# Hybrid encoder trunk on one core: the attention's first tiles on the memory of the decays and shifts, stores of the rotated queries on other queues, the S5 parameters in two parts

## The chip, the cores and the metric

One core of a Trainium2 chip runs the whole layer as one program. The metric is the device time of one execution in microseconds (us). The engines are TensorE (PE, with its weight loads PEld), VectorE (DVE), ScalarE (ACT), GpSimd (POOL) and SyncE (SP, which here only issues DMAs). ACT and POOL can issue DMAs too; each engine's DMAs go out in the order of its own instructions.

## The reference, cut to what matters

One post-norm layer for two groups of tokens that share the weights: 1024 prompt frames and 32 new frames of a running stream (T = 1056 columns).

```python
proj = x @ w_in                       # q_lat 256 | kv_lat 128 | k_rope 32 | u 256 | rwkv 1280
q = rms_norm(q_lat) @ w_qb            # 6 heads x (64 nope + 32 rope), rope columns rotated
ckv = rms_norm(kv_lat); krope = rope(k_rope)
kv = concat(ckv_past, ckv) @ w_kvb    # k_nope and v; past: 512 frames
mla = softmax((q_nope k_nope + q_rope k_rope) * scale) v        # chunk-causal
s5  = glu(S5 recurrence of u)         # parameters: powers of exp(lam * dt), B, C
rwkv = RWKV-7 recurrence of mixes ps = p + (prev - p) * mu      # r, k, v, decay, a, gate
x = layer_norm(alpha * x + concat(mla, s5, rwkv) @ w_out)
x = layer_norm(alpha * x + square(relu(x @ w_up)) @ w_down)
```

All matrix products keep fp32 accuracy: an operand is split into a high and a low part, and three matmuls (high x high, low x high, high x low) take the place of one.

## The kernel before, in words

The program has three stretches. **The input phase** (0 to some 307 us) projects x by column blocks. `in_proj` is 72 matmuls: 8 contraction tiles, three pieces of columns (384, 384 and 288), three matmuls each (lines 63, 65 and 67). `tile_trunk` runs in turn: the input and its split; the S5 parameters (`stage_s5_params`: products `tb` on POOL at line 530, their sum `bl` on VectorE at line 531, four groups of transposes of `bl` on TensorE at line 537, then tables of powers on VectorE, lines 577 to 596); the mix for the low-rank gates and the three k streams; `stage_lora` (line 277); `front_k` for the three pairs of heads (scans of the log decays at line 374 with the mask `m65`, normalisation, the pair products on TensorE at line 725 with their transposes at line 731); the value and receptance streams (`stage_mixed` with q = 2 and 0); the kv latent, the rope key, the q latent and its normalisation; `stage_q`, six products `scq` of q with evictions on ACT (line 1158) and the rotation on POOL (lines 1179 to 1188), stored to the scratch `q_d`; and `stage_u`, two in-projections.

A stream is one `in_proj`, its eviction to `raw` on ACT (lines 225 to 228), a difference on POOL (line 238) and `mix` on VectorE (line 239).

**The middle** (to some 800 us) is the attention beside the two recurrences. `rwkv_inv` is a generator: a substitution of 31 steps on VectorE (lines 759 and 760) up to its yield, then a copy `zt` on ACT, stores to scratch and loads back, and products on TensorE between the attention's (line 786). `side_by_side` alternates steps of the attention (a) and of the streams (b): LEAD steps of a, one of b, then RATIO of a for each of b. The attention starts with `attn_past` (past latents `ct` and past rope keys `kt` are loaded and transposed, lines 1076 and 1082) and `attn_setup` (the keys' rope rows `kr`, the key products `sck` at line 1117, all split into `kh` on ACT and `kl` on VectorE). Rows 96 to 127 of the keys hold a zero block with a row of -1 in it. A `q` of a head is loaded from `q_d` and split into `qh` and `ql`; then scores `sc` come.

**The MLP** is the rest.

A list scheduler sets the order on each engine from the dependencies, with priorities (`high_priority`) and with `issue_after`, which holds a step behind a named instruction. Tiles come from pools, which lie on one another as on a stack. In pools with `reuse_waits="tile"` a new tile waits for the last users of the tiles whose memory it takes; in the others it waits for the pool below.

Of the kernel before, what the change touches and what calls it, by code (L numbers as in the profile page):

```python
# [17 lines left out]
P = 128  # L18
# [392 lines left out]
def stage_s5_params(g, sp):  # L411
# [120 lines left out]
    V.tensor_copy(out=blv[:, :, 7], in_=bbv[0])  # L532
    em = big("em")[:, :2048].rearrange("p (g x) -> p g x", x=P)
# [208 lines left out]
def rwkv_inv(g):  # L742
# [319 lines left out]
RATIO, LEAD, PRIO = 2.5, 24, 120  # L1062
# [3 lines left out]
def attn_past(g):  # L1066

    nc = g.nc
    g.wkv = g.ap0.tile([P, 2, 384], F32, tag="wkv", name="wkv")
    nc.sync.dma_start(out=g.wkv, in_=g.a["w_kvb"])  # L1070
    g.cpast = g.ap0.tile([P, 512], F32, tag="cpast", name="cpast")
    ct = g.ap.tile([P, 4, P], F32, tag="rec", name="ct", bufs=1)
    nc.sync.dma_start(out=ct, in_=g.a["ckv0"].rearrange("(t p) c -> p t c", p=P))
    ps = g.pst.tile([P, 4, P], F32, tag="st", name="sct")
    for t in range(4):
        nc.tensor.transpose(out=ps[:, t], in_=ct[:, t], identity=g.ident)
    nc.scalar.activation(out=g.cpast, in_=ps.rearrange("p t x -> p (t x)"), func=AF.Copy)
    kt = g.ap.tile([P, 4, 32], F32, tag="rt", name="kt", bufs=1)
    nc.sync.dma_start(out=kt, in_=g.a["kr0"].rearrange("(t p) c -> p t c", p=P))
    ps = g.pst.tile([P, 4, P], F32, tag="st", name="sct")  # L1080
    for t in range(4):
        nc.tensor.transpose(out=ps[:32, t], in_=kt[:, t], identity=g.ident)
    g.kpast = g.ap0.tile([P, 512], F32, tag="kpast", name="kpast")[64:96]
    nc.scalar.activation(out=g.kpast, in_=ps[:32].rearrange("p t x -> p (t x)"), func=AF.Copy)


def attn_setup(g):

    nc = g.nc
# [12 lines left out]
    nc.gpsimd.memset(kr[96:97], -1.0)
    split3(g, kr[64:128], g.kh[0][64:128], g.kl[0][64:128])
# [37 lines left out]
def stage_q(g):  # L1141
# [33 lines left out]
    qa = f("qrope")  # L1175
    qs = g.p1.tile([P, 1152], F32, tag="kk", name="qturn", bufs=3)[:, :T]
# [7 lines left out]
    qb, qt = (g.p1.tile([P, 1152], F32, tag="kk", name=x, bufs=3)[:, :T] for x in ("qropeb", "qturnb"))  # L1184
# [110 lines left out]
def side_by_side(g, a, b):  # L1295
# [3 lines left out]
    n, done = LEAD, [False, False]  # L1299
# [335 lines left out]
def tile_trunk(ctx, tc, a, o):  # L1635
# [29 lines left out]
    with ExitStack() as s1:  # L1665
        g.pacc = s1.enter_context(tc.tile_pool(name="pacc", bufs=3, space=PSUM))
        g.pt = s1.enter_context(tc.tile_pool(name="pt", bufs=2, space=PSUM))
        g.wpool = s1.enter_context(tc.tile_pool(name="wpool", bufs=2))
        xp = s1.enter_context(tc.tile_pool(name="xp", bufs=1))
# [5 lines left out]
        g.rawp = s2.enter_context(tc.tile_pool(name="rawp", bufs=1, reuse_waits="tile"))  # L1675
# [4 lines left out]
        lp = s2.enter_context(tc.tile_pool(name="lp", bufs=1, reuse_waits="tile"))  # L1680
        g.at = lp.tile([P, 3, WSH], F32, tag="at", name="at")
        g.cs65 = lp.tile([P, 3, 1073], F32, tag="cs65", name="cs65")
        with tc.tile_pool(name="lq", bufs=1, side="right", reuse_waits="tile") as g.lq:
            with tc.tile_pool(name="s5p", bufs=1, side="right", reuse_waits="tile") as sp:
                stage_s5_params(g, sp)
# [4 lines left out]
            g.lmix = mixed(g, raw_in(g, 3, 9, w=w0), 9)  # L1690
            for p in PAIRS:
                stage_mixed(g, p, 1, w=w1 if p == PAIRS[0] else None)
            stage_lora(g)
# [24 lines left out]
    inv = rwkv_inv(g)  # L1718
    next(inv)
# [143 lines left out]
```

## Time and profile before

| | |
|---|---|
| median of 3 runs | 1632.05 us (1631.82 to 1632.66) |
| the profiled execution | 1634.02 us, span 1632.2 us, 1.8 us around it |
| mean granted TensorE clock | 0.954 |
| busy: PE, DVE, ACT, POOL | 1501.1, 916.5, 512.4, 413.4 us |
| PE's waits of one kind over 7 us in all | `sck` on VectorE 14.9, `pra` on ACT 12.1, `sct` on a DMA 8.4, `av` on POOL 8.3, `acc` on ACT 7.6, `acc` on VectorE 7.2 |

The busy times overlap between engines. A row of a timeline gives the start, the duration, the engine and the line, what is written and read, and in brackets how long the engine stood idle before and what released it. The durations of neighbouring matmuls overlap; their pace is the distance of the starts. SPq and ACTq are the DMA issues of these engines. Clock 1.00 is the full TensorE clock.

### The profile page before, as it was taken

To read this page: it belongs to the slowest core of one execution; us is meant where nothing else is said; L and a number is where in the kernel's file an instruction comes from. 1 tells how busy PE (TensorE), PEld (TensorE's weight loads), DVE (VectorE), ACT (ScalarE), POOL (GpSimd) and SP (SyncE) were. 2 spreads that over 40 slices of the span, in tenths; PEclk is the share of its full clock that TensorE was granted. 3 is DMA by queue.
4 is the path that set the end of the run, shared out by engine and by line. 5 is a ranking of instruction groups with operands and counts; after the bars stand their busy time and mean duration, and the time that the engine had idled before them with its cause. 6 is when DMAs were issued, how large, how long until landed. Compare 5 with 4: busy or idle time off the path is not lost. (4 is left out here: it accounts for less than half of the span.)

```text
span 1632.2 us, 26334 instructions
## 1 busy us (share of the span) xinstructions
PE 1501.1 (92%) x10855; PEld 1348.1 (83%) x10855; DVE 916.5 (56%) x1674; ACT 512.4 (31%) x990; POOL 413.4 (25%) x386
## 2 busy tenths in 40 slices
PE   7899889688899868989799999999999999999995
PEld 6789778466667556657678999999999999999995
DVE  8467958163566534454766755544554545445457
ACT  5434434313554534443223122221111122221122
POOL 3614551622111011121412112221211122212123
PEclk9979999868999989989999999999999999999998
DMA  5314452707233231122612111111111111111012
GB/s 181 124 64 172 139 140 68 186 15 117 61 92 93 58 82 42 60 77 79 204 53 91 39 40 52 52 39 52 40 52 39 39 52 53 51 41 52 14 39 82
DMA packets 112669, 123.50 MB, mean 76 GB/s; under 512 B 51328, under 2 KB 87860, under 8 KB 112168
## 3 DMA queue, kind: packets, MB, share of 16 engines
q1 hardware_dynamic: 93092, 103.64, 21.8%
q10 hardware_dynamic: 19392, 17.97, 3.5%
q8 instruction: 85, 1.39, 0.3%
q14 instruction: 36, 0.29, 0.1%
q0 software_dynamic: 64, 0.20, 0.0%
HBM read 89.05 MB, written 32.68 MB: 75 GB/s over the span
## 5 line engine op out<-in xcount | busy, mean ns | idle before, releaser
L63 PE MATMUL acc<-xh,uphi 128*128 128x384 f32 (+1 forms) x768 | 248.9, 324 | 0.0
L65 PE MATMUL acc<-xl,uphi 128*128 128x384 f32 (+1 forms) x768 | 247.9, 323 | 0.0
L67 PE MATMUL acc<-xh,uplo 128*128 128x384 f32 (+1 forms) x768 | 247.6, 322 | 0.0
L1533 DVE TENSOR_TENSOR rl<-rl 128x384 f32<-128x384 f32 (+1 forms) x96 | 142.1, 1481 | 176.5 <-ACT rl L1532 175.1
L1561 DVE TENSOR_TENSOR yacc<-yacc,acc 128x384 f32<-128x384 f32 (+2 forms) x344 | 158.7, 507 | 111.6 <-PE acc L67 111.6
L63 PE MATMUL acc<-hh,dnhi 128*128 128x384 f32 (+2 forms) x736 | 209.3, 320 | 0.0
L65 PE MATMUL acc<-hl,dnhi 128*128 128x384 f32 (+2 forms) x736 | 207.1, 319 | 0.0
L67 PE MATMUL acc<-hh,dnlo 128*128 128x384 f32 (+2 forms) x736 | 197.4, 319 | 0.0
L50 POOL TENSOR_TENSOR dnlo<-dnraw,dnhi 128x1024 fp32r<-128x1024 f32 x30 | 72.6, 2421 | 337.3 <-ACT dnhi L49 322.1
L63 PEld LDWEIGHTS acc<-xh,uphi 128*128 128x128 f32 x768 | 144.1, 188 | 0.3 <-ACT xh L49 0.3
L67 PEld LDWEIGHTS acc<-xh,uplo 128*128 128x128 f32 x768 | 144.3, 188 | 0.0
L65 PEld LDWEIGHTS acc<-xl,uphi 128*128 128x128 f32 x768 | 144.2, 188 | 0.0
L50 POOL TENSOR_TENSOR uplo<-upraw,uphi 128x1024 fp32r<-128x1024 f32 x34 | 82.3, 2421 | 237.9 <-ACT uphi L49 237.7
L63 PE MATMUL acc<-xh,wmhi 128*128 128x384 f32 (+3 forms) x384 | 134.3, 350 | 8.5 <-ACT xh L49 7.6
L65 PE MATMUL acc<-xl,wmhi 128*128 128x384 f32 (+3 forms) x384 | 134.3, 350 | 2.6 <-DVE xl L50 2.5
L67 PE MATMUL acc<-xh,wmlo 128*128 128x384 f32 (+3 forms) x384 | 133.2, 347 | 0.0
L65 PEld LDWEIGHTS acc<-hl,dnhi 128*128 128x128 f32 x736 | 131.5, 188 | 0.0
L63 PEld LDWEIGHTS acc<-hh,dnhi 128*128 128x128 f32 x736 | 131.4, 188 | 0.0
L67 PEld LDWEIGHTS acc<-hh,dnlo 128*128 128x128 f32 x736 | 128.9, 188 | 0.0
L49 ACT ACTIVATE dnhi<-dnraw 128x1024 fp32r<-128x1024 f32 x30 | 31.8, 1060 | 299.4 <-PE acc L65 249.2
L49 ACT ACTIVATE hh<-rl 128x384 fp32r<-128x384 f32 (+1 forms) x96 | 47.9, 499 | 148.7 <-DVE rl L1533 148.7
L63 PEld LDWEIGHTS acc<-xh,wmhi 128*128 128x128 f32 (+1 forms) x384 | 75.8, 197 | 14.1 <-ACT xh L49 7.9
(484 smaller groups left out, 2897.1 us busy)
## 6 DMA issues: line engine op xcount, KB each, us to landing
upraw<-in_w_up SPq DMA_DIRECT2D x32, 512.0 KB
dnraw<-in_w_dn SPq DMA_DIRECT2D x30, 512.0 KB, 3.6
ld<-rw SPq DMA_DIRECT2D x24, 320.0 KB, 5.8
wmraw<-in_w_m SPq DMA_DIRECT2D x12, 512.0 KB, 4.9
wo<-in_w_out SPq DMA_DIRECT2D x8, 512.0 KB, 4.0
z<-in_xa SPq DMA_DIRECT2D x8, 512.0 KB
out_y<-o SPq DMA_DIRECT2D x8, 512.0 KB, 2.6
xr<-in_xt SPq DMA_DIRECT2D x8, 384.0 KB, 6.5
```

The lines of the kernel that those rows point to most:

```text
L49: nc.scalar.activation(out=hi, in_=ps, func=AF.Copy)
L50: (lo_eng or nc.vector).tensor_tensor(out=lo, in0=ps, in1=hi.bitcast(F32), op=ALU.subtract)
L63: nc.tensor.matmul(out=outs[i], lhsT=lh, rhs=rhs[i][0], start=start, stop=False)
L65: nc.tensor.matmul(out=outs[i], lhsT=lh, rhs=rhs[i][1], start=False, stop=False)
L67: nc.tensor.matmul(out=outs[i], lhsT=ll, rhs=rhs[i][0], start=False, stop=stop)
L1533: nc.vector.tensor_tensor(out=r[:, :n], in0=r[:, :n], in1=r[:, :n], op=ALU.mult)
L1561: nc.vector.tensor_tensor(out=y, in0=y, in1=ps[i][:, :n], op=ALU.add)
```

## The change

Five things change.

1. Pools. `pt` comes below `pacc`; all pools of the phase get `reuse_waits="tile"`. The decays `cs65` and shifts `at`, and then `raw` and `mix`, move to the bottom of the stack, where the attention's first tiles will lie. `ut` leaves `raw`'s pool for `p1`. `p1` (tiles of the k pairs, the mask `m65`) opens when both the S5 and the lora pools have closed.
2. `stage_s5_params` yields ahead of the transposes of `bl`; the rest is issued behind the last matmul of the lora mix and the three k streams.
3. `rwkv_inv` gets a second yield behind the substitution, whose text now stands right behind `front_k`. `zt` and its stores come in the first step of b; the stores go to SP's queue, behind the last SP instruction. LEAD becomes 10, then 14.
4. `attn_past` takes its PSUM from `psc`. `kr` is one tile of 1056 columns with one load, and the keys' rope rows are split from three pieces (past 512, prompt 1024, new 32), with no copy of the past ones into `kr`.
5. `stage_q`: both products of heads 0 to 3's rope columns first, then the first nope product, the rope product of heads 4 and 5, and the other nope products. The nope stores go to ACT's queue, the rope stores to POOL's.

```diff
-        ut = g.rawp.tile([P, L5, NC5], F32, tag="mix", name="ut", bufs=2)
+        ut = g.p1.tile([P, L5, NC5], F32, tag="f", name="ut", bufs=5)
...
     V.tensor_copy(out=blv[:, :, 7], in_=bbv[0])
+    yield
     em = big("em")[:, :2048].rearrange("p (g x) -> p g x", x=P)
...
+    yield
     zt = g.ip.tile([H, 32, 32], F32, tag="nn", name="zt", bufs=1)
     nc.scalar.activation(out=zt, in_=y[:, 0].rearrange("u i a -> u a i"), func=AF.Copy)
-    nc.scalar.dma_start(out=g.zt_d, in_=zt)
-    nc.scalar.dma_start(out=g.xt_d[:, 0:2], in_=y)
+    nc.sync.dma_start(out=g.zt_d, in_=zt)
+    nc.sync.dma_start(out=g.xt_d[:, 0:2], in_=y)
...
-RATIO, LEAD, PRIO = 2.5, 24, 120
+RATIO, LEAD, PRIO = 2.5, (10, 14), 120
...
-    ps = g.pst.tile([P, 4, P], F32, tag="st", name="sct")
+    ps = g.psc.tile([P, 4, P], F32, tag="sc", name="sct")
...
-    kr = g.ap.tile([P, 1568], F32, tag="vo", name="kr", bufs=1)
-    nc.sync.dma_start(out=kr[64:96, 0:TP], in_=g.kr_d[:, 0:TP])
-    nc.sync.dma_start(out=kr[64:96, 1536:1568], in_=g.kr_d[:, TP:T])
-    nc.scalar.activation(out=kr[64:96, 1024:1536], in_=g.kpast, func=AF.Copy)
-    nc.gpsimd.memset(kr[96:128], 0.0)
-    nc.gpsimd.memset(kr[96:97], -1.0)
-    split3(g, kr[64:128], g.kh[0][64:128], g.kl[0][64:128])
+    nc.sync.dma_start(out=kr[64:96], in_=g.kr_d)
+    for x in (kr, g.kpast):
+        nc.gpsimd.memset(x[96:128], 0.0)
+        nc.gpsimd.memset(x[96:97], -1.0)
+    for x, o, c, n in ((g.kpast, TP, 0, 512), (kr, 0, 0, TP), (kr, 1536, TP, TS)):
+        split3(g, x[64:128, c:c + n], g.kh[0][64:128, o:o + n], g.kl[0][64:128, o:o + n])
...
-            nc.sync.dma_start(out=g.q_d[2 * p + h, 0:64], in_=q[hsl(h)])
+            nc.scalar.dma_start(out=g.q_d[2 * p + h, 0:64], in_=q[hsl(h)])
...
+    nope(0)
     for h in range(4):
-        nc.sync.dma_start(out=g.q_d[h, 64:96], in_=qa[32 * h:32 * h + 32])
+        nc.gpsimd.dma_start(out=g.q_d[h, 64:96], in_=qa[32 * h:32 * h + 32])
     product(qb, wr[:, :, 2])
...
+    nope(1)
+    nope(2)
     for h in range(2):
-        nc.sync.dma_start(out=g.q_d[4 + h, 64:96], in_=qb[32 * h:32 * h + 32])
+        nc.gpsimd.dma_start(out=g.q_d[4 + h, 64:96], in_=qb[32 * h:32 * h + 32])
...
+                params = stage_s5_params(g, sp)
+                next(params)
+                g.lmix = mixed(g, raw_in(g, 3, 9, w=w0), 9)
+                for p in PAIRS:
+                    stage_mixed(g, p, 1, w=w1 if p == PAIRS[0] else None)
+                with tc.issue_after(last_traced(g, mybir.EngineType.PE)):
+                    next(params, None)
+                stage_lora(g)
             g.p1 = s2.enter_context(tc.tile_pool(name="p1", bufs=1, reuse_waits="tile"))
...
         for p in PAIRS:
             front_k(g, p)
+        inv = rwkv_inv(g)
+        next(inv)
```

The scheduler's order moves at three places. On TensorE, around the transposes of `bl` (names without `bl` are in-projection matmuls, `fs` is the lora). Before:

```order
L63 MATMUL acc<-xh,wmhi 128x384
L65 MATMUL acc<-xl,wmhi 128x384
L67 MATMUL acc<-xh,wmlo 128x384
L537 MATMUL pt<-ident,bl 128x128 x8
L63 MATMUL acc<-xh,wmhi 128x384
L65 MATMUL acc<-xl,wmhi 128x384
```

Now:

```order
L63 MATMUL acc<-xh,wmhi 128x288
L65 MATMUL acc<-xl,wmhi 128x288
L67 MATMUL acc<-xh,wmlo 128x288
L538 MATMUL pt<-ident,bl 128x128 x8
L277 MATMUL fs<-lah,wh 128x384
L277 MATMUL fs<-lal,wh 128x384
```

252 in-projection matmuls stood ahead of the transposes before; now all 288 of the first four streams do. Two streams later the same order has one more thing: VectorE's scans (line 374) stood behind the mix of the second value stream and now stand behind the third's, and the first product that reads them (line 316) has 612 in-projection matmuls ahead of it instead of 555.

On SP's queue, where the attention's first loads stand. Before:

```order
L1070 DMA wkv<-in_w_kvb 128x768
L1183 DMA q_d<-qrope 32x1056 x4
L1073 DMA ct<-in_ckv 128x4x128
L1079 DMA kt<-in_kr 128x4x32
L1098 DMA kr<-kr_d 32x1024
L1099 DMA kr<-kr_d 32x32
L1198 DMA q<-q_d 96x1056
```

Now (`in_w_u` are weights of the last in-projections; `wkv` stands four rows higher):

```order
L55 DMA wmraw<-in_w_u 128x1024
L1075 DMA ct<-in_ckv 128x4x128
L1081 DMA kt<-in_kr 128x4x32
L1100 DMA kr<-kr_d 32x1056
L936 DMA st<-in_s 128x3x64
L628 DMA ces<-tab_d 128x2x536
L983 DMA gate<-rw_61 128x32
L983 DMA gate<-rw_62 128x32
L983 DMA gate<-rw_63 128x32
L1202 DMA q<-q_d 96x1056
L765 DMA zt_d<-zt 108x1024
```

No store of q stands on this queue any more, and the stores of the inverse stand behind the first load of a `q`.

On POOL, from the rotation of q to the attention's clearings. Before:

```order
L1181 TENSOR_TENSOR qrope<-qrope,qturn 128x1056
L1186 TENSOR_TENSOR qturnb<-qropeb,ropes 64x1056
L1187 TENSOR_TENSOR qropeb<-qropeb,ropec 64x1056
L1101 MEMSET kr 32x1568
L1213 MEMSET mx 128x18 x2
L637 MEMSET ces 128x8
L1188 TENSOR_TENSOR qropeb<-qropeb,qturnb 64x1056
L1102 MEMSET kr 1x1568
L1109 TENSOR_TENSOR qh<-kr 32x1056
```

Now:

```order
L1183 TENSOR_TENSOR qrope<-qrope,qturn 128x1056
L1189 TENSOR_TENSOR qropeb<-qropeb,ropec 64x1056
L1186 DMA q_d<-qrope 32x1056 x4
L1188 TENSOR_TENSOR qturnb<-qropeb,ropes 64x1056
L1190 TENSOR_TENSOR qropeb<-qropeb,qturnb 64x1056
L1194 DMA q_d<-qropeb 32x1056 x2
L1102 MEMSET kr 32x1056
L1217 MEMSET mx 128x18 x2
L1130 MEMSET vo 128x13x64
L638 MEMSET ces 128x8
L1103 MEMSET kr 1x1056
L1111 TENSOR_TENSOR qh<-kr 32x1056
```

The clearing of `kr` now stands behind six DMA issues. On TensorE the products of q stood among the 72 matmuls of the last `u`; now all of them stand ahead of these.

## Rows read from the trace of the kernel before

**Rows 1.** Windows of the span: busy us of each engine, PE clock, DMA share, GB/s.
```profile
63.30:68.00 4.70, 4.70 (x20) 4.70 (x21) 0.28 (x1) 1.19 (x2) 4.38 (x4) 0.60 0.28 92
...
246.00:307.10 61.10, 60.99 (x312) 51.12 (x310) 34.08 (x58) 23.11 (x49) 12.72 (x5) 1.00 0.40 108
307.10:333.50 26.40, 7.46 (x17) 3.52 (x16) 13.92 (x13) 9.94 (x18) 25.95 (x17) 0.61 0.53 157
...
800.00:1600.00 800.00, 798.50 (x4954) 781.96 (x4953) 435.52 (x698) 176.14 (x326) 171.77 (x83) 1.00 0.16 49
```

**Rows 2.** Waits of TensorE over the whole span: us in total, times, longest us.
```profile
PE sck L1117 <- DVE kl L50: 14.9, 5, 7.4
...
PE sct L1076 <- DMA ct<-in_ckv: 8.4, 1, 8.4
```

**Rows 3.** Timeline of TensorE around the transposes of `bl`.
```profile
53.71 0.34 PE L67 MATMUL acc<-xh,wmlo 128*128 128x384 f32 x1
53.89 0.34 PE L63 MATMUL acc<-xh,wmhi 128*128 128x384 f32 x1
...
63.23 1.97 PE L537 MATMUL pt<-ident,bl 128*128 128x128 f32 x8 [6.02 <-DVE bl L531]
```

**Rows 4.** Timeline of VectorE, the sum `bl`.
```profile
57.63 5.55 DVE L531 TENSOR_TENSOR bl<-bl,tb 128x1792 f32<-128x1792 f32 x1 [3.56 <-POOL tb L530]
```

**Rows 5.** Timeline of VectorE, the scans and the mix ahead.
```profile
137.54 1.31 DVE L239 SCALAR_TENSOR_TENSOR mix<-mix,vec,raw 128x1058 f32<-128x1058 f32 x1
139.62 11.36 DVE L374 TENSOR_TENSOR_SCAN cs<-m,cs 128x260 f32<-128x260 bf16 x14 [0.77 <-POOL m L1689]
```

**Rows 6.** Timeline of ACT, last evictions of the second and third value streams.
```profile
130.44 0.19 ACT L228 ACTIVATE raw<-acc 128x32 f32<-128x32 f32 x1
...
144.46 0.19 ACT L228 ACTIVATE raw<-acc 128x32 f32<-128x32 f32 x1
```

**Rows 7.** Timeline of TensorE, the first pair products.
```profile
178.64 1.16 PE L725 MATMUL fs<-fc,fq 64*64 64x64 f32 x64 [1.66 <-DVE fq L344]
```

**Rows 8.** Timeline of SP, its DMA issues after the input phase.
```profile
307.65 3.55 SPq L1183 DMA_DIRECT2D q_d<-qrope  x4
311.25 0.51 SPq L1073 DMA_DIRECT2D ct<-in_ckv  x1
```

**Rows 9.** Timeline of TensorE, start of the attention.
```profile
315.56 1.09 PE L1076 MATMUL sct<-ident,ct 128*128 128x128 f32 x4 [8.44 <-DMA ct<-in_ckv]
...
333.55 0.44 PE L63 MATMUL sc<-kh,qh 128*128 128x128 f32 x1 [1.72 <-DVE kl L50]
```

**Rows 10.** Window of the q products alone (PE, PEld, ACT; clock, DMA share, GB/s).
```profile
269.94:307.10 37.16, 23.62 (x72) 12.93 (x72) 7.91 (x18) 1.00 0.54 145
```

**Rows 11.** Timeline of POOL, rotation of q, clearing of `kr`, rows of `qh`.
```profile
299.88 2.44 POOL L1179 TENSOR_TENSOR qrope<-qrope,ropec 128x1056 f32<-128x1056 f32 x1 [37.28 <-ACT qturn L1158]
...
312.31 1.40 POOL L1101 MEMSET kr<- 32x1568 f32 x1
...
317.86 1.94 POOL L1109 TENSOR_TENSOR qh<-kr 32x1056 fp32r<-32x1056 f32 x1
```

**Rows 12.** Groups of POOL: busy us, mean ns, idle before, releaser.
```profile
L1733 POOL DMA_DIRECT2D mg_d<-yc x1 | 0.9, 942 | 0.3 <-POOL yc L992 0.3
```

**Rows 13.** Timeline of ACT, the split of `kr`.
```profile
321.14 1.51 ACT L49 ACTIVATE kh<-kr 64x1568 fp32r<-64x1568 f32 x1
```

**Rows 14.** Timeline of VectorE, residuals of q and of the keys.
```profile
318.72 4.01 DVE L50 TENSOR_TENSOR ql<-q,qh 96x512 fp32r<-96x512 f32 x2 [37.54 <-ACT qh L49]
322.66 0.67 DVE L50 TENSOR_TENSOR kl<-sck,kh 64x512 fp32r<-64x512 f32 x1
323.36 2.83 DVE L50 TENSOR_TENSOR kl<-kr,kh 64x1568 fp32r<-64x1568 f32 x1
```

**Rows 15.** Instructions on the mixes: durations ns, first and last start us.
```profile
L344 POOL TENSOR_TENSOR mix<-mix,cs x6: 240/1784/3149, 201.3 to 218.3; 128x1024 f32<-128x1024 f32 x3, 128x32 f32<-128x32 f32 x3
...
L337 ACTq DMA_DIRECT2D rw<-mix x3: 397/397/443, 206.6 to 221.3; - x3
```

More of the change, by code (lines that the diff above doesn't have):

```diff
@@ L1079, in attn_past @@
     nc.sync.dma_start(out=kt, in_=g.a["kr0"].rearrange("(t p) c -> p t c", p=P))
-    ps = g.pst.tile([P, 4, P], F32, tag="st", name="sct")
+    ps = g.psc.tile([P, 4, P], F32, tag="sc", name="sct")
     for t in range(4):
         nc.tensor.transpose(out=ps[:32, t], in_=kt[:, t], identity=g.ident)
-    g.kpast = g.ap0.tile([P, 512], F32, tag="kpast", name="kpast")[64:96]
-    nc.scalar.activation(out=g.kpast, in_=ps[:32].rearrange("p t x -> p (t x)"), func=AF.Copy)
+    g.kpast = g.ap0.tile([P, 512], F32, tag="kpast", name="kpast")
+    nc.scalar.activation(out=g.kpast[64:96], in_=ps[:32].rearrange("p t x -> p (t x)"), func=AF.Copy)
 def attn_setup(g):
@@ L1090, in attn_setup @@
     g.kh, g.kl, g.q2 = [], [], []
+    kr = g.ap.tile([P, T], F32, tag="q", name="kr", bufs=1)
     for i in range(NKT):
@@ L1165, in stage_q, with nope @@
             nc.scalar.dma_start(out=wr[:, k, j, x:x + 32 * n].rearrange("p (h c) -> p h c", c=32), in_=g.a["w_qb"][:, k, h:h + n, c:c + 32])
-    for p in range(3):
+    def nope(p):
         q = f("qnope")
@@ L1174, in stage_q @@
         nc.scalar.dma_start(out=sn[32 * h:32 * h + 32], in_=g.a["rope"][32:64])
-    qa = f("qrope")
-    qs = g.p1.tile([P, 1152], F32, tag="kk", name="qturn", bufs=3)[:, :T]
+    qa, qs, qb, qt = (g.p1.tile([P, 1152], F32, tag="kk", name=x, bufs=3)[:, :T] for x in ("qrope", "qturn", "qropeb", "qturnb"))
     product(qa, wr[:, :, 0])
@@ L1181, in stage_q @@
     nc.gpsimd.tensor_tensor(out=qa, in0=qa, in1=qs, op=ALU.add)
+    nope(0)
     for h in range(4):
-        nc.sync.dma_start(out=g.q_d[h, 64:96], in_=qa[32 * h:32 * h + 32])
-    qb, qt = (g.p1.tile([P, 1152], F32, tag="kk", name=x, bufs=3)[:, :T] for x in ("qropeb", "qturnb"))
+        nc.gpsimd.dma_start(out=g.q_d[h, 64:96], in_=qa[32 * h:32 * h + 32])
     product(qb, wr[:, :, 2])
@@ L1298, in side_by_side @@
     mark = None
-    n, done = LEAD, [False, False]
+    n, k, done = LEAD[0], 0, [False, False]
     def step(i, x):
@@ L1311, in side_by_side @@
         if not done[1]:
-            with g.tc.high_priority(PRIO):
+            with g.tc.high_priority(PRIO), g.tc.issue_after(last_traced(g, mybir.EngineType.SP)) if k == 0 else nullcontext():
                 step(1, b)
             g.scan_dve = last_traced(g, DVE)
-        n += RATIO
+        k += 1
+        n += LEAD[k] if k < len(LEAD) else RATIO
 def stage_attn(g):
@@ L1665, in tile_trunk @@
     with ExitStack() as s1:
[L1666 to L1669, printed above, removed]
+        g.pt = s1.enter_context(tc.tile_pool(name="pt", bufs=2, space=PSUM, reuse_waits="tile"))
+        g.pacc = s1.enter_context(tc.tile_pool(name="pacc", bufs=3, space=PSUM, reuse_waits="tile"))
+        lp = s1.enter_context(tc.tile_pool(name="lp", bufs=1, reuse_waits="tile"))
+        g.cs65 = lp.tile([P, 3, 1073], F32, tag="cs65", name="cs65")
+        g.at = lp.tile([P, 3, WSH], F32, tag="at", name="at")
+        g.rawp = s1.enter_context(tc.tile_pool(name="rawp", bufs=1, reuse_waits="tile"))
+        g.wpool = s1.enter_context(tc.tile_pool(name="wpool", bufs=2, reuse_waits="tile"))
+        xp = s1.enter_context(tc.tile_pool(name="xp", bufs=1, reuse_waits="tile"))
         g.xh = xp.tile([P, KD, T], F32R, tag="xh", name="xh")
@@ L1674, in tile_trunk @@
         g.kq = s2.enter_context(tc.tile_pool(name="kq", bufs=1, reuse_waits="tile"))
-        g.rawp = s2.enter_context(tc.tile_pool(name="rawp", bufs=1, reuse_waits="tile"))
         stage_x(g)
@@ L1679, in tile_trunk @@
         nc.sync.dma_start(out=g.msk, in_=a["msk"])
-        lp = s2.enter_context(tc.tile_pool(name="lp", bufs=1, reuse_waits="tile"))
-        g.at = lp.tile([P, 3, WSH], F32, tag="at", name="at")
-        g.cs65 = lp.tile([P, 3, 1073], F32, tag="cs65", name="cs65")
         with tc.tile_pool(name="lq", bufs=1, side="right", reuse_waits="tile") as g.lq:
             with tc.tile_pool(name="s5p", bufs=1, side="right", reuse_waits="tile") as sp:
-                stage_s5_params(g, sp)
+                params = stage_s5_params(g, sp)
[6 more added lines that the diff above has]
+                stage_lora(g)
             g.p1 = s2.enter_context(tc.tile_pool(name="p1", bufs=1, reuse_waits="tile"))
@@ L1689, in tile_trunk @@
             nc.gpsimd.memset(g.m65[:, 0:260:65], 0.0)
[L1690 to L1693, printed above, removed]
             log_exp_table(g, g.table)
@@ L1717, in tile_trunk @@
     g.pst = spr.enter_context(tc.tile_pool(name="pst", bufs=2, space=PSUM, reuse_waits="tile"))
-    inv = rwkv_inv(g)
-    next(inv)
     g.ap = sa.enter_context(tc.tile_pool(name="ap", bufs=1, reuse_waits="tile"))
```

## Prediction

> **What bounds the kernel now.** I read the windows of the span first [rows 1]. From 800 us to 1600 us TensorE is busy 798.50 of 800 us at a clock of 1.00: the MLP is at its floor, and the diff leaves it alone. From 246 to 307.1 it is busy 60.99 of 61.10 us. From 307.1 to 333.5, where the attention begins, it is busy only 7.46 of 26.40 us, at a mean granted clock of 0.61 (1.00 is 2.4 GHz, 0.50 is 1.2 GHz). So I look for holes of TensorE before 400 us, and the list of its waits [rows 2] names the two largest causes in that place: the key products behind VectorE's residuals `kl` (14.9 us in five waits) and the transposes behind the load of `ct` (8.4 us). A third hole lies early: at 63.23 us TensorE has stood 6.02 us for `bl` of the S5 parameters [rows 3]. The run with these rows took 1634.02 us; my sum is made on it and taken off the median, 1632.05 us, which is 1.97 us (0.12%) lower. No change that I count is smaller than 0.2% (3.3 us), about the least that a measurement of this kernel can tell.
>
> **The S5 transposes (minus 5.3, then partly lost).** VectorE starts `bl` at 57.63 us, when POOL's products are ready, and takes 5.55 us [rows 4]. TensorE reaches the transposes at 57.21 us (63.23 less 6.02 [rows 3]) with 36 input-projection matmuls still behind them. The new order puts these first. Their pace is 0.18 us at 384 columns (53.71 to 53.89 [rows 3]); 12 are that wide and 24 have 288 columns, so 12 x 0.18 + 24 x 0.13 = 5.3 us of work go into the 6.02 us hole. After the hole, 20 matmuls took 4.70 us at a clock of 0.60 [rows 1], where full clock would need about 3.5: another 1.2 us at most.
>
> The price stands in the next stage. The scans on VectorE started at 139.62 us, behind the mix of the second value stream at 137.54 [rows 5]; now the mix of the third stands ahead of them. The third stream's last eviction was at 144.46 us, and the second's at 130.44 [rows 6], so the second needed 7.1 us from eviction to its mix. With 5.3 us saved the third is evicted at 139.2, mixed at 146.3 and the scans start at 147.6: 8.0 us later than now. Against that, TensorE has 57 more input-projection matmuls (612 for 555) to do before it asks for the scans' first results, 57 x 0.165 = 9.4 us. Now it waits 1.66 us for that chain at 178.64 [rows 7]. What is left after that point is 9.4 us shorter, and the point itself comes 8.0 us later, so the input phase ends 1.4 us earlier; if POOL isn't busy with a weight when the third stream arrives, the delay is 4.6 and the gain is back at 4.8. A gain above 6.5 (5.3 + 1.2) is excluded, and I take **3 us**, the middle; the ends are 0 and 6.5.
>
> **The substitution.** In VectorE's order its 62 instructions stand at the same places between the normalisations as before; only its issue in the text moved. Its ACT copy `zt` and the two stores behind it move from ACT's queue to SP's, behind the first load of `q`; the inverse's loads follow them, and their matmuls come only after head 0's scores. I count nothing: the cover is the 33 us of products and `u` between. If the copy is late, the evictions behind it on ACT hold the products, which is a rival below.
>
> **The attention's start (minus 15.4).** Now: the input phase ends at 307.1 us; SP first issues four stores of the rotated q (307.65, 3.55 us in all), and only then `ct` at 311.25 [rows 8]; TensorE gets it at 315.56, and scores begin at 333.55 [rows 9]: 26.4 us after the end. After: `wkv`, `ct`, `kt` and `kr` are issued ahead of every load of q, into memory whose last readers are done long before, so the first 8.44 us of that are gone. What is late next? I follow both chains from S, the first q product.
>
> POOL's chain. The six products take 23.62 us of TensorE at most [rows 10], about 3.6 us each without the overlaps, and the 72 matmuls of the last `u` 11.6 us, so `u` ends at about S + 33.5. The rope products go first; with one block of the first nope product between, their evictions are done at S + 9. POOL then does three operations of 2.44 us [rows 11] (S + 16.3), one more (S + 18.7), issues four stores, does two more operations, issues two stores, and clears `kr` and `vo`. The only DMA that POOL issued itself took 0.94 us there [rows 12]; six cost 5.7 us. The clearing of 32 x 1568 took 1.40 us [rows 11], so 0.94 for 1056, twice, and some 1.2 for the rest: S + 18.7 + 4.9 + 5.7 + 3.1 = S + 32.4. That is 1.1 us before `u` ends, so POOL is just covered. The Trainium skill (DMA: Bandwidth & Descriptors, "Anatomy of one DMA") gives about 2.0 us of fixed cost for a DMA issued from GpSimd and does not say how much of it holds the engine; were it all of it, an estimate from that page, six would cost 12.0 us and POOL would end 5.2 us after `u`. The one row speaks for the smaller price.
>
> VectorE's and ACT's chain from the end of `u`, T. Transpose and eviction of `ct` to T + 1.1; then ACT splits `kr` (1.51 us for 1568 columns [rows 13], 1.0 for 1024), T + 2.1; VectorE's residual took 2.83 us for 1568 [rows 14], so 1.9 for 1024 and 0.9 for `kpast`, T + 4.9; six residuals of 0.67 [rows 14] and two short ones make T + 9.3, and the `ql` of head 0, 2.0 us as now beside POOL [rows 14], T + 11.3. TensorE itself needs some 5 us for its transposes and key products in that time. So scores start **11 us** after T instead of 26.4: minus 15.4. The ends: minus 21 if only TensorE's own 5.4 us remain; minus 6 if POOL's chain ends 9 us later than I have it. The clock will be low again at the first scores, since TensorE still stands for some 6 us; I count 1 us back of what is now lost.
>
> The sum is 3 + 15.4 + 1 = 19.4 us: 1632.05 - 19.4 = **1612.6 us**. Behind head 0 the order of TensorE is the same and its waits shift along.
>
> **Rivals.** (a) *The wait moves to POOL or stays on VectorE.* POOL's operations of 2 to 2.4 us and VectorE's with two inputs slow one another (2.0 us for a 96 x 512 residual against 0.67 for 64 x 512 [rows 14]), and the four `qh`/`ql` rows on POOL from 317.86 [rows 11] now meet the same residuals. For it: POOL is covered by 1.1 us only. The hole gives 6 to 9, the S5 part 1 to 3: minus 7 to minus 12, about 1622 us. The Trainium skill (SBUF — State Buffer, "two separate sides") has it as an exclusive lock of a shared port pair, and says that POOL cannot write the descriptors of its own DMAs while VectorE holds it; by that rule six stores could be held, the trace agrees on the operations, and no row shows the stores.
> (b) *More than the sum.* The early gain stays whole (6.5) and scores start about 6 us after T: minus 27, 1605 us. For it: much of ACT's and VectorE's work could run sooner than its order tells; against it, `kr`'s split stands behind `cpast` on ACT.
> (c) *The tiles still wait.* Where the attention's tiles lie on memory of something late, `ct` comes no earlier, and the rest is worth 0 to 3 us: 1630 to 1632. Against it: the decays are last read from 218.3 us, and the mixes' last store is issued at 221.3 us [rows 15], over 80 us before.
> (d) *Slower: the front stage waits for memory.* The tiles of the k pairs and the mask of the scans are now allocated after all S5 and lora tiles, so the mask's clearing on POOL stands behind a further stream. If the scans start later than 139.62 + 9.4 = 149 us, each us beyond delays the whole input phase; the case turns slower when they start after 149 + 16.4 = 165 us. One stream of 72 matmuls lasts 11.6 us, so it takes two more streams ahead of them than I count (147.6 + 11.6 = 159 is not enough, 170.8 is): 5.4 us longer, about 1637 us. For it: every tile allocated later can only wait for more; against it: now the scans wait only 0.77 us for the mask [rows 5].
>
> **How the numbers follow.** My forecast (gains of 14 to 24 us) 0.55; (a) 0.20; (b) 0.12; (c) 0.06; (d) 0.07. Faster is forecast, (a) and (b): 0.87; same is (c), 0.06; slower is (d), 0.07. The range reaches from (b)'s 1605 with some reserve, 1601, to the small end of (a) with both terms at their low ends, 1627.
>
> **What would show it.** Right: the wait of 6.02 us for `bl` is below 1 us; no wait on the load of `ct`; `q_d` stores on POOL of about 0.9 us; scores some 11 us after the last `u` matmul, with waits on `kl` of 5 to 8 us in place of 14.9. Wrong, in the first term, if the scans start after 149 us or TensorE's wait before the pair products is over 4 us; in the second, if scores still start over 18 us after `u`; and the whole if a new wait of over 5 us stands between 400 and 800 us, where I count none.

## The result and the profile after

The changed kernel takes 1616.64 us (median of 4 runs, 1609.90 to 1621.15), against 1632.36 us of the kernel before in the same session (4 runs, 1631.82 to 1638.51): ratio 0.9892, 95% interval 0.985 to 0.9934; the medians lie 15.7 us apart. Run again later (e1, six runs from 1609.57 to 1613.23, with the wait of 10.2 us shown below) it took 1611.65 us, ratio 0.9879 (0.9849 to 0.9909). The forecast, 1612.6 us, lies between the two medians. Its working doesn't hold: one term was 10 us too small, another 5 us too large, a cost of 10 us stood at nothing, and 9 us came from a place that I had called unchanged. The profiled execution of the change took 1609.90 us, the fastest of its four; its span is 1608.1 us, 24.1 less than that of the profile before.

The windows of the changed kernel, in the columns of [rows 1]:

```profile
63.30:68.00 4.70, 4.61 (x29) 3.92 (x30) 0.19 (x2) 0.00 (x0) 4.51 (x5) 1.00 0.24 86
246.00:306.50 60.50, 47.02 (x213) 35.58 (x212) 41.30 (x56) 18.72 (x42) 19.49 (x13) 0.92 0.23 60
306.50:322.30 15.80, 5.74 (x16) 2.12 (x14) 8.80 (x12) 7.78 (x16) 15.51 (x13) 0.75 0.46 137
```

The stretch behind the hole is at full clock now. The start of the attention has shrunk from 26.4 to 15.8 us. But in the 60.5 us ahead of it TensorE is busy only 47.02 us, where it had been busy 60.99 of 61.10. Its list of waits names most of the cause (columns as in [rows 2]):

```profile
PE scq L1159 <- ACT qnope L1160: 10.2, 1, 10.2
PE sck L1119 <- DVE kl L50: 9.8, 4, 4.9
```

TensorE's timeline, for [rows 3, 9]:

```profile
63.40 1.09 PE L538 MATMUL pt<-ident,bl 128*128 128x128 f32 x8 [1.19 <-DVE bl L531]
...
71.58 1.60 PE L538 MATMUL pt<-ident,bl 128*128 128x128 f32 x8 [2.61 <-ACT em L539]
...
290.73 4.10 PE L1159 MATMUL scq<-qn,wqa 128*128 128x288 f32 x8 [10.23 <-ACT qnope L1160]
...
306.30 0.60 PE L1078 MATMUL sct<-ident,ct 128*128 128x128 f32 x4
...
316.35 2.04 PE L1119 MATMUL sck<-cpast,wkv 128*128 128x512 f32 x2 [4.93 <-DVE kl L50]
...
322.36 0.45 PE L63 MATMUL sc<-kh,qh 128*128 128x128 f32 x1 [3.33 <-POOL kl L1109]
```

The wait of 6.02 us for `bl` is 1.19 (with 2.61 between two groups of transposes), the load of `ct` is waited for no longer, and a new hole of 10.23 us stands in the products of q. It follows from ACT's queue and the end of the substitution on VectorE:

```profile
288.36 1.94 ACT L764 ACTIVATE zt<-y 108x1024 f32<-108x1024 f32 x1 [12.17 <-DVE y L761]
290.20 1.24 ACT L1160 ACTIVATE qnope<-scq 128x384 f32<-128x384 f32 x3
```

```profile
140.06 7.54 DVE L374 TENSOR_TENSOR_SCAN cs<-m,cs 128x260 f32<-128x260 bf16 x15
...
269.76 0.52 DVE L760 TENSOR_TENSOR tmp<-y,nn 108x350 f32<-108x350 f32 x1
...
275.60 2.59 DVE L761 TENSOR_TENSOR y<-y,tmp 108x312 f32<-108x312 f32 x1
278.23 2.54 DVE L760 TENSOR_TENSOR tmp<-y,nn 108x270 f32<-108x270 f32 x1
280.80 0.44 DVE L761 TENSOR_TENSOR y<-y,tmp 108x270 f32<-108x270 f32 x1
...
288.06 0.26 DVE L761 TENSOR_TENSOR y<-y,tmp 108x62 f32<-108x62 f32 x1
```

The scans started at 140.06, not at 147.6. The substitution's last step is over only at 288.3 us, `zt` waits for it with ACT idle 12.17 us, and the evictions of q stand behind `zt`. The lateness is POOL's, which now rotates q in just this time:

```profile
275.31 2.55 POOL L1183 TENSOR_TENSOR qrope<-qrope,qturn 128x1056 f32<-128x1056 f32 x1
277.80 2.67 POOL L1189 TENSOR_TENSOR qropeb<-qropeb,ropec 64x1056 f32<-64x1056 f32 x1
280.42 2.16 POOL L1186 DMA_DIRECT2D q_d<-qrope  x4
...
288.96 0.97 POOL L1102 MEMSET kr<- 32x1056 f32 x1
306.59 0.17 POOL L1217 MEMSET mx<- 128x18 f32 x2 [16.65 <-PE acc L67]
...
307.59 0.97 POOL L1103 MEMSET kr<- 1x1056 f32 x1
308.64 1.95 POOL L1111 TENSOR_TENSOR qh<-kr 32x1056 fp32r<-32x1056 f32 x1
```

An instruction of the substitution over 312 or 270 columns takes 2.5 to 2.6 us beside POOL's operations, and 0.44 once POOL issues DMAs (280.42). e12, whose POOL starts the rotation only at 285.53 us, shows the same instructions undisturbed:

```profile
269.73 0.52 DVE L760 TENSOR_TENSOR tmp<-y,nn 108x350 f32<-108x350 f32 x1
...
275.37 0.28 DVE L761 TENSOR_TENSOR y<-y,tmp 108x62 f32<-108x62 f32 x1
```

From the same start the last 14 instructions take 18.6 us in the change and 5.9 in e12. These 12.6 us are as long as ACT's wait ahead of `zt`.

The last rows of POOL, in the timeline above, show a wait that I had not seen: it is done with its stores and `kr` at 289.9, and then stands 16.65 us, since the memory of `mx` is read by the last matmul of u. The rows of `qh` come after that, and the first load of `q`, whose tile takes the memory of `kr`, after them, on SP:

```profile
277.70 0.40 SPq L1075 DMA_DIRECT2D ct<-in_ckv  x1
297.46 0.38 SPq L1081 DMA_DIRECT2D kt<-in_kr  x1
...
317.88 0.32 SPq L1202 DMA_DIRECT2D q<-q_d  x1
```

**The clock of the input phase**, which I had not read beyond 68 us. Windows of before (columns of [rows 1]):

```profile
95.00:100.00 5.00, 5.00 (x25) 4.10 (x24) 2.32 (x4) 1.82 (x4) 0.00 (x0) 0.78 0.27 111
100.00:105.00 5.00, 5.00 (x15) 3.37 (x14) 1.36 (x3) 1.60 (x4) 3.41 (x4) 0.50 0.30 114
105.00:110.00 5.00, 5.00 (x14) 4.04 (x14) 4.46 (x23) 0.58 (x1) 1.37 (x2) 0.50 0.30 100
110.00:115.00 5.00, 5.00 (x23) 4.15 (x23) 1.65 (x3) 0.87 (x2) 0.00 (x0) 0.84 0.00 0
115.00:120.00 5.00, 5.00 (x20) 4.54 (x19) 2.54 (x14) 1.34 (x3) 0.26 (x3) 0.67 0.27 108
```

The same of the change:

```profile
95.00:100.00 5.00, 5.00 (x20) 4.45 (x20) 4.83 (x9) 0.95 (x2) 3.88 (x4) 0.66 0.31 105
100.00:105.00 5.00, 5.00 (x29) 3.98 (x27) 4.90 (x13) 1.55 (x3) 0.26 (x3) 1.00 0.10 39
105.00:110.00 5.00, 5.00 (x28) 4.08 (x29) 4.38 (x11) 0.58 (x2) 0.00 (x0) 1.00 0.26 105
```

TensorE is busy 5.00 of 5.00 us in each, so the list of waits and the busy share tell nothing. Before, the clock is at 0.50, the lower level, for 10 us and between the levels on both sides: the busy time times what is missing to 1.00, 5 x (0.22 + 0.50 + 0.50 + 0.16 + 0.33) = 8.6 us, is lost. After, 5 x 0.34 = 1.7 us (the windows to 120 us are at 1.00).

**ACT's order at the Gelu of the S5 part**, at 600 us. Before, ACT:

```profile
595.40 1.28 ACT L682 ACT_TABLE_LOAD   x1 [9.11 <-DMA zt<-z_d]
596.70 1.98 ACT L682 ACTIVATE zt<-zt 128x2128 f32<-128x2128 f32 x1
598.69 1.28 ACT L76 ACT_TABLE_LOAD   x1
599.98 0.87 ACT L881 ACTIVATE wu<-prw 128x512 f32<-128x512 f32 x2
```

TensorE:

```profile
600.63 1.54 PE L831 MATMUL pra<-ld 64*64 64x128 f32 x12 [12.08 <-ACT wu L881]
```

ACT waits 9.11 us for a load, and `wu` stands behind it; TensorE waits 12.1 us for that. After, `wu` goes ahead:

```profile
574.64 0.87 ACT L883 ACTIVATE wu<-prw 128x512 f32<-128x512 f32 x2
...
584.76 1.28 ACT L683 ACT_TABLE_LOAD   x1 [3.35 <-DMA zt<-z_d]
```

The edit doesn't touch these lines; the scheduler placed them anew.

### The profile page after: what moved, and what is told of

It is laid out like the page before. It is cut to its first block, busy times and chain, and to the rows that moved or that the text cites. A ratio compares the mean times of both kernels' runs of the same rounds, so it can differ in the third digit from the quotient of the medians.

```text
span 1608.1 us, 26358 instructions
## 1 busy us (share of the span) xinstructions
PE 1487.7 (93%) x10855; PEld 1336.1 (83%) x10855; DVE 920.6 (57%) x1676; ACT 510.6 (32%) x991; POOL 415.9 (26%) x394
## 5 line engine op out<-in xcount | busy, mean ns | idle before, releaser
L65 PE MATMUL acc<-xl,wmhi 128*128 128x384 f32 (+3 forms) x384 | 130.2, 339 | 1.6 <-DVE xl L50 1.6
L67 PE MATMUL acc<-xh,wmlo 128*128 128x384 f32 (+3 forms) x384 | 129.6, 338 | 0.0
```

What stands on the lines that cost most here:

```text
L65: nc.tensor.matmul(out=outs[i], lhsT=lh, rhs=rhs[i][1], start=False, stop=False)
L67: nc.tensor.matmul(out=outs[i], lhsT=ll, rhs=rhs[i][0], start=False, stop=stop)
```

## The experiments

The table gives each kernel's median, its ratio to the kernel before as measured in the same session (there 1632.36 to 1635.13 us), and starts from its profiled execution in us: T is the last matmul of u, then the first scores (with their distance from T), the seventh and eighth group of `pra`, and the span.

| kernel | median | ratio (95%) | T | scores | pra 7 | pra 8 | span |
|---|---|---|---|---|---|---|---|
| before | 1632.36 | 1 | 306.83 | 333.55 (26.7) | 587.68 | 643.71 | 1632.2 |
| the change | 1616.64 | 0.9892 (0.985, 0.9934) | 306.17 | 322.36 (16.2) | 576.12 | 623.12 | 1608.1 |
| e1, the same again | 1611.65 | 0.9879 (0.9849, 0.9909) | 304.60 | 320.57 (16.0) | 572.02 | 618.61 | 1607.8 |
| e2 | 1605.76 | 0.9839 (0.9811, 0.9867) | 294.17 | 310.07 (15.9) | 570.34 | 616.69 | 1603.3 |
| e4 | 1604.14 | 0.9832 (0.98, 0.9864) | 294.44 | 309.27 (14.8) | 564.20 | 610.95 | 1598.1 |
| e5 | 1622.32 | 0.9931 (0.9906, 0.9955) | 306.94 | 334.21 (27.3) | 591.43 | 636.70 | 1625.4 |
| e6 | 1621.08 | 0.9928 (0.9904, 0.9953) | 308.44 | 324.68 (16.2) | 574.51 | 627.49 | 1612.6 |
| e7 | 1609.59 | 0.9851 (0.9825, 0.9877) | 305.23 | 321.38 (16.2) | 575.12 | 619.74 | 1607.8 |
| e8 | 1600.58 | 0.9799 (0.9774, 0.9825) | 291.18 | 306.13 (15.0) | 564.28 | 610.79 | 1601.8 |
| e9 | 1625.44 | 0.9953 (0.9934, 0.9972) | 301.59 | 324.05 (22.5) | 587.80 | 640.67 | 1630.9 |
| e10 | 1640.37 | 1.0047 (1.0029, 1.0065) | 314.57 | 335.95 (21.4) | 599.50 | 651.67 | 1643.4 |
| e11 | 1602.13 | 0.981 (0.9784, 0.9836) | 292.84 | 311.53 (18.7) | 568.39 | 614.95 | 1600.4 |
| e12 | 1611.10 | 0.9863 (0.9846, 0.988) | 293.91 | 320.97 (27.1) | 577.75 | 630.21 | 1615.3 |

### e2: the copy `zt` behind q's evictions

```diff
+    with g.tc.issue_after(g.q_done):
         nc.scalar.activation(out=zt, ...)
...
         stage_q(g)
+        g.q_done = last_traced(g, mybir.EngineType.Activation)
```

> The ACT copy zt of the inverse stands behind the last q store instead of in front of the nope evictions; nothing else moves on any engine. Theory 1 (zt held ACT's queue for 12.2 us behind the substitution, and TensorE 10.2 us behind the evictions): that wait is gone, the last u ends at 296 to 298 us instead of 306.3, scores start 7 to 10 us sooner, and the time falls by 7 to 10 us against the changed kernel. Rival (that wait covers POOL's and SP's chain to the first q load, which then takes its place): u ends sooner by 10 us but the scores by less than 3, and the time falls by less than 3 us.

The wait of 10.23 us is gone, T comes 10.4 us earlier than in e1, the scores 10.5. That is the price of the copy, shown. The median fell by only 5.9 us. In the two profiles the stretch from the scores to `pra` 7 is 8.8 us longer in e2, and most of that is the clock: it costs 21.7 us there for 15.2 in e1 (summed as above over windows of 5 us; the last section shows two of them).

### e3 and e4: POOL's fills behind the rows of `kr`

```diff
+    for x in g.q2[0] + g.q2[1]:
+        nc.gpsimd.tensor_tensor(out=x[96:128], ...)
+    g.kr_set = last_traced(g, mybir.EngineType.Pool)
...
+    with g.tc.issue_after(g.kr_set):
         nc.gpsimd.memset(vo[:, :, 1], 1.0)
...
+    with g.tc.issue_after(g.kr_set):
         nc.gpsimd.memset(mx, -3.0e38)
```

> On POOL the row of -1 of kr and the four zero rows of qh and ql stand ahead of the clearings of mx and vo, which wait for the last u matmul (16.65 us idle in the trace). Theory 1 (the first q load waits for these four operations, since q takes kr's memory, and the residuals of VectorE run beside them): the operations run before 300 us, kl of kr takes 1.3 us instead of 3.85 for both pieces, the q load is issued at 311 to 313 us instead of 317.9, scores start 3 to 5 us sooner: minus 3 to 5 us against the changed kernel. Rival (the key residuals on VectorE and ACT end last anyway): scores move by less than 1.5 us.

1612.24 us, ratio 0.9874 (0.9844 to 0.9905): no difference from e1, and no verdict on the theory, for the edit didn't do what was meant. The clearing of `ces` (line 638), whose memory the last matmul of u reads too, had taken the place of `mx`, and POOL waited 16.49 us there. e4 has this edit and that of e2.

> Both edits together. If the two waits are in series, as theory 1 has them: minus 11 to 14 us against the changed kernel, 1600 to 1604 us. If one covers the other: no more than the larger of the two alone.

T is as in e2 and the scores come 1.1 us sooner after it; the medians of the two can't be told apart. POOL still waits 4.32 us at `ces` here, so this run doesn't test the theory either.

### e8 and e11: `ces` too, then the stores back on SP

e8 is e4 with the clearing of `ces` behind `kr_set`; e11 is e8 with all stores of q on SP's queue.

> As the kernel with both edits, and the clearing of ces (which waits for the last u matmul and stood ahead of kr's row on POOL) behind the rows too. Theory 1 (POOL's four operations on kr hold the first q load and slow VectorE's residual of kr): kr's row is set at 290 us, the four operations end by 301 us, the residual of kr takes 1.3 us for both pieces instead of 3.5, the first q load is issued at 299 to 302 us instead of 305.2, scores start at 305 to 307 us instead of 309.3: minus 2 to 4 us against the kernel with both edits. Rival (VectorE and ACT splitting the key products end last): under 1 us.

> The best version so far (copy zt behind the evictions of q, POOL's fills behind the rows of kr and qh) with all twelve stores of q on SP's queue, none on POOL's and ACT's. Theory 1 (POOL's six DMA issues, 3.2 us, are on the path to the first q load): kr's rows and the rows of qh end some 3 us earlier, scores begin 11 to 12 us after the end of u in place of 14.8, time 1596 to 1599. Rival 2 (they are not on it; VectorE's residuals and the loads set the start): 1599 to 1603, scores 14 to 16 us after the end of u.

e8 has the lowest median, 2.0% under before. POOL's `kr` row is at 287.20, ahead of T, and still the scores come 15.0 us after T (14.8 in e4), as the rival has it: VectorE's residuals meet the POOL operations that now lie at the same place. In e11 POOL sets `kr` 1.7 us earlier (285.53), but the last stores of q wait for an eviction behind `zt`, and `ct` behind them on SP. TensorE and VectorE there:

```profile
299.66 1.09 PE L1080 MATMUL sct<-ident,ct 128*128 128x128 f32 x4 [6.53 <-DMA ct<-in_ckv]
```

```profile
302.49 1.33 DVE L50 TENSOR_TENSOR kl<-kr,kh 64x1024 fp32r<-64x1024 f32 x2 [13.79 <-ACT kh L49]
```

So neither expectation holds for the scores (18.7 us after T); the medians can't be told apart. With POOL idle the two residuals take 1.33 us; in the change, beside POOL, 3.85. From the transposes of `ct` on, the scores come after 11.9 us in e11, 14.8 in e8 and 16.1 in the change; the prediction's 11 us is about what the chain takes without POOL, though in e11 all else had 6.5 us more to get ready.

### e5: before, with the Gelu late

```diff
-    log_exp_table(g, [...AF.Gelu_apprx_tanh...], False)
+    with g.tc.issue_after(last_traced(g, mybir.EngineType.Activation)):
+        log_exp_table(g, [...AF.Gelu_apprx_tanh...], False)
```

> The kernel before with one thing moved: on ACT, the table load and the Gelu of the S5 output (which wait for the load of zt from scratch) stand behind wu of the recurrence and the next block's copies, as they do in the changed kernel, instead of in front of wu. Theory 1 (of the 24 us between the two profiled spans some 10 come from this move, which the scheduler made by itself): TensorE's wait of 12.1 us for wu is gone, 8 to 12 us off the kernel before. Rival (the recurrence's chain is late at that point anyway, or the attention's matmuls stand behind another wait): less than 3 us.

Theory 1 holds. Three ACT instructions move. From `pra` 7 to `pra` 8 it takes 45.3 us instead of 56.0 (the change: 47.0), the wait of 12.1 us is gone, and the run is 11 us shorter by the ratio. The order at the Gelu alone is worth that much.

### e6: the change, with the S5 parameters in one part

```diff
-                next(params)
+                list(params)
...
-                with tc.issue_after(last_traced(g, mybir.EngineType.PE)):
-                    next(params, None)
```

> The changed kernel with the S5 parameters in one part again, ahead of the lora mix and the k streams. Theory 1 (the early hole costs what it shows): TensorE waits about 6 us for bl at 57 to 63 us again, the input phase ends 3 to 6 us later, plus 3 to 6 us against the changed kernel. Rival (the copy zt on ACT sets the end of the input phase, at the end of the substitution, not TensorE): the wait is back but the input phase ends within 2 us of the changed kernel, and the time too.

The wait of 5.99 us for `bl` is back, and so is the low clock from 95 to 120 us, at 0.77, 0.50, 0.50, 0.84 and 0.68. Yet T is only 2.3 us later: with the input phase later, the substitution is over before the evictions queue (it ends at 280.7 us), and the wait for `zt` has vanished. From `pra` 7 to 8 it takes 53.0 us, 6.0 more than in the change, since the Gelu has moved again. By the ratios e6 is some 6 to 8 us slower than the change, so theory 1 is right about the hole, and the rival about the input phase but for 0.3 us, and not about the time. (The profiled run of e6, the fastest of its nine, gains 3.9 us between the scores and `pra` 7, where the clock costs it 8.9 us for 15.5.)

### e12: before, with the S5 parameters in two parts

> The kernel before with the S5 parameters in two parts as in the change (and the pool of the k pairs opened behind them); nothing else. Between 95 and 120 us the kernel before runs TensorE at 0.50 to 0.84 of its clock while it is busy without a break, and every kernel with the split runs that stretch at 1.00 or nearly. Theory 1 (the split takes this low stretch away, wherever else the kernel is as before): the clock is 1.00 in the windows from 100 to 120 us, the wait of 6.0 us for the sum bl falls to about 1.2, the last matmul of u starts 8 to 12 us earlier (295 to 299 us), and the time is 7 to 12 us less than that of the kernel before (ratio 0.993 to 0.996). Rival 2 (the low stretch has another cause, and the split is worth the hole alone): the clock from 100 to 118 us is near 0.5 as before, u ends 1 to 4 us earlier, ratio 0.998 to 1.0.

The windows:

```profile
95.00:100.00 5.00, 5.00 (x19) 4.36 (x19) 4.90 (x7) 1.24 (x3) 4.28 (x4) 0.68 0.33 105
100.00:105.00 5.00, 5.00 (x29) 4.18 (x28) 4.85 (x14) 1.55 (x3) 0.26 (x3) 0.97 0.00 0
105.00:110.00 5.00, 5.00 (x28) 4.13 (x27) 4.30 (x7) 0.58 (x2) 0.00 (x0) 1.00 0.27 111
```

and TensorE at the first pair products [rows 7] and at the attention's start:

```profile
177.46 1.16 PE L726 MATMUL fs<-fc,fq 64*64 64x64 f32 x64 [0.16 <-DVE fq L344]
...
303.87 1.09 PE L1077 MATMUL sct<-ident,ct 128*128 128x128 f32 x4 [9.66 <-DMA ct<-in_ckv]
```

Theory 1 holds for the clock: the low stretch is gone with the split alone, as it came back in e6 without the split. T comes 12.9 us earlier, and the time falls by 22.6 us (1633.70 to 1611.10), about twice what I expected and as much as by the whole change (ratio 0.9863; the change 0.9892 and 0.9879). So what the rest of the change gains, its own costs take back. Not all of the 22.6 us is the split's place in the input phase: the Gelu moved here too, and `pra` 7 to 8 is 52.5 us for 56.0. In the profile, the slowest of the four runs (1617.08), the end comes 16.9 us earlier; where the other 5.7 us of the medians lie stays open. The start of the attention is that of before (27.1 us, with 9.66 us for `ct`).

### e7, e9 and e10: the queues and the place in memory

e7 is the change with q's stores back on SP. e9 is the change with the pools of `cs65`, `at`, `raw` and `mix` back on the second stack. e10 is before with these pools moved as in the change.

> The changed kernel with all stores of q on SP's queue again, ahead of ct and kt there; nothing else of the change undone, TensorE's order the same. Theory 1 (the loads came early because their memory is free early; the queue alone would not have stopped them long, since the rotation on POOL ends before u does): ct is issued at 286 to 292 us, before u ends at 305, no wait for ct, the time within 2 us of the changed kernel; POOL is 3 us shorter. Rival (the queue was the cause): ct comes after u's end, TensorE waits over 4 us for it, plus 5 us or more.

> Only the places of the pools of the decays, shifts, raw and mix are put back to the second stack, over the weights and the split input; order of the text, stores on ACT and POOL, two-part S5 and early substitution stay. Theory 1 (the place in memory is what lets the attention's loads go early): ct is issued only after the last matmul of u (307 us and later), TensorE waits 5 us or more for it, scores begin 22 to 27 us after the end of u, and the time is 6 to 11 us over that of the change: 1619 to 1626. Rival 2 (the new order of the products and the queues does it, with any placement): ct is there before u ends, scores 16 us after the end of u, 1609 to 1614.

> The kernel before with only the pools moved as in the change (and reuse of memory by tile). Theory 1 (the place in memory alone is enough): ct is issued before 300 us, no wait of TensorE on it, scores 15 to 18 us after the end of u, 1621 to 1625. Rival 2 (memory and order are both needed): ct still stands on SP's queue behind the four stores of the rotated q, whose sum POOL ends only around 307 us; the wait of about 8 us for ct stays, scores about 25 us after the end of u, 1629 to 1634.

e7 changes nothing that the ratios can tell: `ct` is issued at 297.47, later than theory 1 had it (286 to 292) and yet ahead of T, and isn't waited for. In e9 it is issued at 302.38, behind T (301.59), and TensorE waits:

```profile
308.19 1.12 PE L1078 MATMUL sct<-ident,ct 128*128 128x128 f32 x4 [6.31 <-DMA ct<-in_ckv]
```

The scores come 22.5 us after T instead of 16.2: the place in memory is worth 6.3 us there, as theory 1 has it. The whole time isn't its price, though: T is 4.6 us earlier than in the change (the wait behind `zt` was 4.14 us in that order), and most of what e9 lost lies later: `pra` 7 to 8 is 52.9 us, as the Gelu moved, and from the scores to `pra` 7 it takes 10.0 us more than the change, nearly all of it clock (25.0 us lost there for 15.5; TensorE stands 1.3 us longer). Its profiled run is the slowest of the twelve. In e10 `ct` goes out right behind the four stores of the rotated q (305.82, then `ct` at 307.58), as rival 2 says. TensorE doesn't wait for it all the same, for T was 7.7 us later (314.57), with a wait of 4.32 us on the evictions of `qrope`, and the run was slower than rival 2 had it. So e10 doesn't measure the memory by itself. Of the 10.5 us that the start of the attention gained, e9 shows 6.3 to be the place in memory, in this order of products; the other 4.2 (26.7 to 22.5) no run takes apart.

## Why the prediction was right, and where not

- **The S5 term (3 us, "a gain above 6.5 is excluded"): the failed step.** Alone it gives 12.9 us at T (e12), and in the change without the copy's wait 12.7 (e2). What I missed is the clock: I read it from 63.3 to 68 us only, and 8.6 us were lost at 95 to 120 us, of which 1.7 are left. (At the hole itself little is gained: the waits are 1.19 and 2.61 for 6.02, where the prediction asked for under 1, and a new low stretch at 73 to 83 us takes 3 to 3.4 us in the change and e12.) Up to T, TensorE stands 5.6 us less in e12 than before and loses 5.1 us less to the clock (windows of 2 us: 31.6 and 16.2 us before, 26.0 and 11.1 in e12). The price was wrong too: with the clock up, the third stream was evicted at 134.33 us in the change, not at 139.2, and mixed 4.5 us later, not 7.1, so the scans started at 140.06. The 57 matmuls, 9.4 us by my own pace, that moved ahead of the pair products were done when these began, after a wait of 0.16 us, at 177.46 in e12 (178.64 before). That is 9.4 + 1.2 = 10.6 of the 12.9, with the wait of 1.66 us in it; behind them a wait of 3.9 us is gone, and 3.7 us on `qn` are new. My two cases, 1.4 and 4.8, were both too low.
- **"I count nothing" for the substitution: failed.** The cover, TensorE's products, needed evictions that stood behind `zt` on ACT. I named this as a thing to fear, but gave it no place among the rivals and no price. It is 10.2 us, and it ate the S5 gain: T moved by 0.7 us only. The copy was late because POOL's rotation, which the new order of the products brings forward, meets the substitution on VectorE (18.6 us for 5.9); I had this slowing in rival (a), for the attention's start alone.
- **The attention's start (minus 15.4): right in kind, 4.9 too large.** T to scores fell from 26.7 to 16.2, minus 10.5. `ct` was no longer waited for (e9 against the change). A POOL DMA took 0.54 us of the engine (2.16 for four), not 0.94, and POOL reached 289.9, which is the S + 32.4 of the working. But I had it free to go on, and it waited for the last matmul of u. Rival (a) had the rest: waits on `kl` of 9.8 us in place of my 5 to 8, with residuals of 3.85 us beside POOL (7.5 in e11, with 1.33). The Trainium skill (SBUF — State Buffer, "two separate sides") calls this an exclusive lock of a shared port pair; the trace agrees for the operations (0.44 and 2.54 us, 1.33 and 3.85). The stores were not held in a way that shows. The Trainium skill names that hold, in the same section, for VectorE operations in a 2-port mode, a condition that the prediction left out. The Trainium skill (DMA: Bandwidth & Descriptors, "Anatomy of one DMA") has about 2.0 us of fixed cost for a GpSimd DMA and puts most of it down to completion, not to the issue, which the prediction left out. Its 12.0 us for six DMAs, an estimate from that page's figure, was no price for the engine; in this trace the six keep POOL 3.2 us.
- **"Behind head 0 the order of TensorE is the same and its waits shift along": failed.** ACT's order moved at the Gelu, and the stretch from `pra` 7 to 8 became 9.0 us shorter (e5 measures such a move at 11 us). The prediction's test asked for new waits there, and the change shows in one that is gone.
- **The sum.** In the two profiles: 0.7 at T, 10.5 at the scores, 9.0 at the Gelu and 3.9 elsewhere make 24.1; the medians differ by 15.7. My 19.4 came of errors that cancelled; the 1 us for the clock at the first scores can't be told apart.
- Rivals (c) and (d) did not occur: `ct` went out at 277.70, and the scans started 8.9 us under the 149 us from which they would have cost.

## What to carry to other kernels

Read the granted clock in windows of 5 us over the whole program, also where an engine is 100% busy: a low stretch there is lost time that no wait names. An instruction whose issue is moved in the text must be followed on its own in-order queue, with what stands behind it; "covered" holds only if the cover doesn't pass through that queue. And where a scheduler sets the order, compare the order of all engines to the end, not at the edited place alone.

## What the runs showed of the hardware

A low stretch of the clock can be a fixed feature of a program's order: from 95 to 120 us, before, e5, e6 and e10 all run at 0.50 for 10 us, while the change, e2, e7, e9 and e12 lose 1.8 us or less there. In before TensorE had been busy 4.77 of 5.00 us from 63 to 68 and all of the time from there; in the change it had small holes to 73 us (busy 2.39 of 5.00 from 68 to 73) and was at 0.50 from 73 to 78. The split moves the lora's products too: from 85 to 98 us, just ahead of the drop, 34 matmuls of line 277 take 5.71 of TensorE's 13.00 us in before, and 30 take 4.98 in e12, where the clock fell as well (0.68 from 95 to 100) but was back at 0.97 in the next 5 us. No run moves these without the transposes, so why the clock stays low in the one and not in the other remains open.

Other stretches change from run to run. From 345 to 350 us the same program shows 0.52 in the profile of the change and 1.00 in that of e1, and from 95 to 100 us 0.66 and 1.00. After the first scores, e2 ran at 0.50 where e4, with nearly the same order, ran at 1.00. e2:

```profile
330.00:335.00 5.00, 4.44 (x70) 3.11 (x69) 2.83 (x8) 0.00 (x0) 0.00 (x0) 0.50 0.01 3
335.00:340.00 5.00, 5.00 (x77) 4.61 (x76) 3.37 (x7) 0.00 (x0) 0.00 (x0) 0.50 0.02 3
```

e4:

```profile
330.00:335.00 5.00, 3.79 (x110) 3.12 (x110) 4.19 (x10) 0.00 (x0) 0.00 (x0) 1.00 0.01 3
335.00:340.00 5.00, 5.00 (x131) 4.60 (x125) 2.42 (x6) 1.79 (x3) 0.00 (x0) 1.00 0.18 30
```

That is 5 us between single executions, and the runs of one kernel lie 3.7 to 15.0 us apart, so the profile of one execution can't be read finer than that here.
